# Two attention heads side by side on the column halves of the array: probabilities times v, denominators from sums, and another order in a pair

## The chip, the cores and the metric

The kernel runs on one core of a Trainium2 chip. The metric is the time on the device in microseconds (us), the median of several runs. A core has TensorE (PE, matrix products, with its weight loads as PEld), VectorE (DVE), ScalarE (ACT), GpSimd (POOL) and queues for transfers (SP is the one that loads weights). Products land in eight banks of PSUM; the other engines read them from there.

## The reference, cut to what matters

Two layers: retention and a feed-forward net, then attention and a feed-forward net, each followed by a LayerNorm with residual, for 512 tokens of 1024 channels. The change is in attention, which has 16 heads of 64 channels, and in each head three groups with dilations 1, 4 and 16:

```python
for g, (window, dil) in enumerate(DILATED_PAIRS):
    o, lse = _dilated_group(proj[0, g], proj[1, g], proj[2, g], rel_bias[...], window, dil)
    outs.append(o)
    lses.append(lse)
w = jax.nn.softmax(jnp.stack(lses, axis=0), axis=0)
o = jnp.sum(w[..., None] * jnp.stack(outs, axis=0).astype(jnp.float32), axis=0)
```

Merging the groups by their log-denominators is the same as one softmax over all keys of the three groups: sum of exp(s − m) times v, divided by the sum of exp(s − m). That is how the kernel does it.

## The kernel before, in words

**Split weights.** Every large product is done in three: a number is split into hi (a copy by ACT) and lo (the rest, by DVE), and hi·hi, hi·lo and lo·hi are added in PSUM (`mm3`). A weight arrives raw (`wraw`, SP), ACT writes `whi` (L84), DVE `wlo` (L85); this is done two tiles ahead of use, with four buffers for the halves. A tile against all tokens (`wstat`) is 8 × 3 = 24 products of 128x512 on PE.

**Attention** runs over eight pairs p of two heads, in an order that `att_schedule` writes out. The steps of a pair: *scores* of group 0, 1 and 2 (`head_mms`, the two heads on the two row halves of the array, hi and lo as above; DVE adds the position tables and keeps a running maximum `mx`); *top* for each head (PE transposes `mx`, DVE reduces it, and the maximum of each token is put on a diagonal: `diaghi` by DVE, `diaglo` by ACT, one buffer of each); *exp* for each head (two products with ones spread the maxima into a bank, DVE subtracts it from the scores in four instructions, ACT takes exps in three); *pv* (exps times v); *norm* (reciprocal of the denominator, product, split into `zhi` and `zlo`). The projections q and k of the next pair (`qk`, six weight tiles a pair) and v of the next four heads (`v`) are put between these steps, so that PE has work while DVE and ACT are at the scores. Group n = 1 and 2 of a pair need the q and k that qk 2 to 5 make, with two sets of q and k buffers that alternate (q0, k0 and q1, k1).

**pv before.** The stationary operand is 128 columns: 64 of v and 64 of ones, so that half of a bank gets the sum and the other half the denominator. A head has twelve products in float: eight over 128 columns (two groups, four residues), and four over 256, 256, 256 and 128.

**The output projection** multiplies z by two weights for each two pairs: *o*(q) fetches the weights of pairs 2q and 2q + 1, *rows*(q, b) does block b of 128 tokens (12 products of 128x512, both halves of the channels), and DVE adds the result to the residual r. The rows of pairs 0 and 1 stand in pair 4, those of pairs 2 and 3 in pair 7. The rest is done behind the loop, in `rows_product` over pairs 4 to 7, where each block's LayerNorm follows directly (`ln`: DVE statistics, POOL's power for rs at L254, ACT's scale at L281, POOL's addition at L282). The blocks are r_77 to r_80; PE transposes each (L298) for the feed-forward net, whose first products then start on halves of the tokens (128x256).

Of the kernel before, what the change touches and what calls it, by code (L numbers as in the profile page):

```python
# [7 lines left out]
F32 = mybir.dt.float32  # L8
F32R = mybir.dt.float32r
AF = mybir.ActivationFunctionType  # L10
ALU = mybir.AluOpType
# [4 lines left out]
P = 128  # L16
D = 1024
T = 512
# [6 lines left out]
HD = 64  # L25
# [7 lines left out]
RES = 4  # L33
# [1 line left out]
PH = 3 * RUN  # L35
W0, W1, W2 = (2 * RES - 1) * PH, 256, 256
WB = W0 + W1 + W2
VW = 3 * HD
S0 = 7 * P


# [56 lines left out]
def trunk(tc, a, out):  # L98
    nc = tc.nc
    plan = []  # L100

    def ret_plan(h):
        qk = [(a["w_rqk"], 4 * h + i) for i in range(4)]
        v = [(a["w_rv"], 4 * h + i) for i in range(4)]
        g = [(a["w_rg"], 4 * h + i) for i in range(4)]
        o = [(a["w_ro"], 4 * h + i) for i in range(4)]
        return qk, v, g, o

    def ffn_plan(i):
        f = 0  # L110
        for n in FC:
            plan.extend((a[f"w_up{i}"], 2 * f + j) for j in range(2 * n))
            plan.extend((a[f"w_dn{i}"], f + j) for j in range(n))
            f += n

    rp = [ret_plan(h) for h in range(RH)]
    plan += rp[0][0] + rp[0][1]
    for h in range(RH):
        plan += rp[h][2]
        if h + 1 < RH:  # L120
            plan += rp[h + 1][0] + rp[h + 1][1]
        plan += rp[h][3]
    ffn_plan(0)
    tiles = {
        "qk": lambda p, i: [(a["w_aqk"], 6 * p + i)],
        "v": lambda q, g: [(a["w_av"], 6 * q + 2 * g + i) for i in range(2 + 2 * g)],
        "o": lambda q, _: [(a["w_ao"], 2 * q + i) for i in range(2)],
    }
    first, steps = att_schedule()
    for kind, *at in first + [s for t in steps for s in t]:  # L130
        if kind in tiles:
            plan += tiles[kind](*at)
    plan += tiles["o"](2, 0) + tiles["o"](3, 0)
    ffn_plan(1)

    with tc.tile_pool(name="const", bufs=1) as cpool, tc.tile_pool(
        name="xpool", bufs=1
    ) as xpool, tc.tile_pool(name="wraw", bufs=2) as wraw, tc.tile_pool(
        name="whl", bufs=4
    ) as whl, tc.tile_pool(name="lnp", bufs=2) as lnp, tc.tile_pool(  # L140
        name="ps", bufs=8, space=PSUM
    ) as ps, tc.tile_pool(name="scratch", bufs=1, space=DRAM) as dr:
        ws = Weights(nc, plan, wraw, whl, 2, 1)
        c = Core(nc, tc, a, out, ws, cpool, xpool, lnp, ps, dr)
        c.retention()
        c.ffn(0)
        c.attention(first, steps)
        c.ffn(1)


def att_schedule():


    first = [("qk", 0, i) for i in range(4)] + [("v", 0, g) for g in range(2)]
    steps = []
    for p in range(8):
        gaps = [[("qk", p, 4), ("qk", p, 5)], [], [], [], []]
        if p < 7:
            gaps[1] += [("qk", p + 1, 0)]
            gaps[2] += [("qk", p + 1, 1)]  # L160
            gaps[3] += [("qk", p + 1, 2)]
            gaps[4] += [("qk", p + 1, 3)]
            if p % 2 and p // 2 < 3:
                for g in range(2):
                    gaps[2 + g].append(("v", p // 2 + 1, g))
        if p in (4, 7):
            q = 0 if p == 4 else 1
            gaps[1].append(("o", q, 0))
            for b, g in enumerate((1, 2, 3, 4) if p == 4 else (2, 2, 3, 4)):
                gaps[g].append(("rows", q, b))  # L170
        t = [("scores", p, 0)] + gaps[0] + [("scores", p, 1)] + gaps[1] + [("scores", p, 2)]
        t += gaps[2] + [("top", p, 0), ("top", p, 1)]
        t += gaps[3] + [("exp", p, 0)] + gaps[4]
        t += [("exp", p, 1), ("pv", p, 0), ("pv", p, 1), ("norm", p, 0)]
        steps.append(t)
    return first, steps


def residue(t, r):


    return t.rearrange("p (j r l) -> p r j l", j=NB, r=RES)[:, r]


class Core:
# [388 lines left out]
    def attention(self, first, steps):  # L574
        nc, tc = self.nc, self.tc
        with tc.tile_pool(name="at", bufs=1) as at:
            self.at = at
            self.ones = at.tile([P, P], F32R, name="ones")
            nc.vector.memset(self.ones.bitcast(F32), 1.0)
            self.vt = [at.tile([P, 12, VW], F32, name=f"v{i}") for i in range(3)]  # L580
            for v in self.vt:
                nc.gpsimd.memset(v[:, :, HD : 2 * HD], 1.0)
            self.qt, self.kt = (
                [[at.tile([P, T], F32R, name=f"{w}{i}{n}") for n in ("hi", "lo")] for i in range(2)]
                for w in "qk"
            )
            self.zs, self.wo, self.pv = {}, {}, {}
            self.tabs = {0: self.bias_tables(0)}
            n = sum(k == "qk" for k, *_ in first)
            for (_, p, i), bk in zip(first[:n], self.wstat_many(n)):  # L590
                self.att_qk(p, i, bk)
            for t in [first[n:]] + steps:
                for kind, x, y in t:
                    getattr(self, "att_" + kind)(x, y)
            tabs = [at.tile([P, 2, 4 * P], F32, name="tab", bufs=2) for _ in range(2)]
            self.ln_params(2, *[t.rearrange("p h c -> p (h c)") for t in tabs])
            self.rows_product([self.zs[p] for p in range(4, 8)], False, True)

    def bias_rows(self):

# [66 lines left out]
    def att_v(self, quad, g):  # L667


        n = 2 if g else 1  # L670
        banks = [self.bank() for _ in range(2 * n)]
        per = 4 // n
        for i in range(2 * n):
            w = self.ws.get()
            for j in range(per):
                k = per * i + j
                c = slice(j * 256 * n, (j + 1) * 256 * n)
                if g:
                    xk = [self.at.tile([P, T], F32R, name=f"xr{m}", bufs=3) for m in ("hi", "lo")]
                    for t, x in zip(xk, (self.xhi, self.xlo)):  # L680
                        self.nc.gpsimd.tensor_copy(
                            out=t.rearrange("p (r j l) -> p r j l", r=RES, j=NB),
                            in_=x[:, k, :].rearrange("p (j r l) -> p r j l", j=NB, r=RES),
# [3 lines left out]
                for b in range(NB):  # L687
                    bk = banks[b] if g else banks[b // 2]
                    o = 0 if g else b % 2 * 256
# [7 lines left out]
        for pr in range(2):  # L697
            v = self.vt[(2 * quad + pr) % 3]
            for b, bk in enumerate(banks):
                src = bk.rearrange("p (b x) -> p b x", b=2)[:, :, pr * P : (pr + 1) * P]  # L700
                dst = v[:, 4 + b : 12 : 4] if g else v[:, 2 * b : 2 * b + 2]
                for hh in range(2):
                    self.nc.scalar.activation(
                        dst[:, :, 2 * hh * HD : (2 * hh + 1) * HD],
                        src[:, :, hh * HD : (hh + 1) * HD],
                        AF.Copy,
                    )

    def head_mms(self, banks, cols, ks, qs, start, stop):

# [115 lines left out]
        tt(out=own[:, 0:3, P : 2 * P], in0=own[:, 0:3, P : 2 * P], in1=mb[:, 1:4], op=ALU.subtract)  # L826
        nc.scalar.activation(s[:, 0:S0], s[:, 0:S0], AF.Exp)

    def att_pv(self, p, h):

        bk = self.bank()
        c = slice(h * HD, h * HD + P)
        s, v = self.s[:, h], self.vt[p % 3]
        for g in (1, 2):
            for r in range(4):
                self.mm(residue(bk, r), v[:, 4 * g + r, c], residue(s[:, S0 + (g - 1) * T : S0 + g * T], r),
                        g == 1 and r == 0, False)
        for J in range(NB):
            n = 2 * P if J < 3 else P
            self.mm(bk[:, J * P : J * P + n], v[:, J, c], s[:, 2 * J * P : 2 * J * P + n], False, J == 3)  # L840
        self.pv[h] = bk

    def att_norm(self, p, _):
        nc, at = self.nc, self.at
        b0, b1 = self.pv[0], self.pv[1]
        parts = NB if p == 7 else 1
        den = at.tile([P, T], F32, name="den")
        zf = at.tile([P, T], F32, name="zf")
        hi = at.tile([P, T], F32R, name="zhi", bufs=5)
        lo = at.tile([P, T], F32R, name="zlo", bufs=5)  # L850
        nc.scalar.activation(den[0:HD], b0[HD:P], AF.Copy)
        nc.scalar.activation(den[HD:P], b1[0:HD], AF.Copy)
        for c in range(parts):
            c = slice(c * T // parts, (c + 1) * T // parts)
            nc.vector.reciprocal(out=den[:, c], in_=den[:, c])
            for bk, hs in ((b0, slice(0, HD)), (b1, slice(HD, P))):
                nc.vector.tensor_tensor(out=zf[hs, c], in0=bk[hs, c], in1=den[hs, c], op=ALU.mult)
            self.split(hi[:, c], lo[:, c], zf[:, c])
        self.zs[p] = (hi, lo)

# [120 lines left out]
```

## Time and profile before

| | us |
|---|---|
| median of 3 runs | 1708.4 (1707.71 to 1708.44) |
| profiled execution | 1707.9 |
| its span in the trace | 1705.8 |
| mean granted clock of PE | 0.997 of full |
| PE busy | 1691.8 |

The span is what the trace covers; the 2.1 us around it belong to the run's time. The clock's share is of the higher of PE's two levels, 2.4 GHz; 0.50 is 1.2 GHz.

### The profile page before, as it was taken

What the parts mean: (1) busy time and instruction counts of PE and PEld (TensorE: products, weight loads), DVE (VectorE), ACT (ScalarE), POOL (GpSimd) and SP (SyncE); (2) the same over time, 40 slices, a digit from 0 to 9 for tenths busy, and PEclk for the clock granted to TensorE, in tenths of its full rate; (3) what the DMA queues carried; (4) which work ended last, traced back from release to release, by engine and by line L of the source; (5) the groups of instructions that cost most, each with busy time, mean ns of one, the idle gap of its engine ahead of it and who ended that gap; (6) DMA issues with size and microseconds to landing.
All of it is one profiled execution on the core that took longest, in us unless ns stands there. A gap on an engine that the chain in (4) does not pass through costs nothing.

```text
span 1705.8 us, 20490 instructions
## 1 busy us (share of the span) xinstructions
PE 1691.8 (99%) x8548; PEld 1422.7 (83%) x8548; DVE 829.5 (49%) x1111; ACT 523.0 (31%) x777; POOL 188.3 (11%) x269
## 2 busy tenths in 40 slices
PE   9999999999999999999999999999999999999998
PEld 7888888888888888889888888888888888888886
DVE  6454553657433243336364564564478733233335
ACT  4322232323322122213242342432443422212221
POOL 0000000003000000017323123122100200000002
PEclk9999999999999999999999999999999999999999
DMA  7322222222223222223313223223221322223221
GB/s 275 132 74 82 73 99 76 98 74 99 99 99 99 99 99 99 98 75 115 101 58 112 75 64 110 75 87 98 76 87 62 114 90 93 99 76 122 99 99 50
DMA packets 47548, 162.52 MB, mean 95 GB/s; under 512 B 5268, under 2 KB 7316, under 8 KB 47456
## 3 DMA queue, kind: packets, MB, share of 16 engines
q1 hardware_dynamic: 42144, 155.80, 26.2%
q0 software_dynamic: 5312, 5.42, 1.8%
q8 instruction: 67, 1.10, 0.3%
q14 instruction: 25, 0.20, 0.0%
HBM read 159.02 MB, written 2.17 MB: 94 GB/s over the span
## 4 chain that ended last, share of the span: by engine, by line
PE 90%; issue 7%; DVE 2%; POOL 1%; ACT 0%; DVEq 0%; ACTq 0%; POOLq 0%
PE bank L202 89%; DVE wlo L85 1%; PE bank L298 0%; PE bank L531 0%; PE bank L784 0%; POOL r L282 0%; DVE r L284 0%; DVE r L275 0%; DVE r L317 0%; POOL rs L254 0%; DVE st L265 0%; ACT whi L84 0%; ACT r L281 0%; DVE xlo L206 0%; DVEq L974 0%
## 5 line engine op out<-in xcount | busy, mean ns | idle before, releaser
L85 DVE TENSOR_TENSOR wlo<-wraw,whi 128x1024 fp32r<-128x1024 f32 (+1 forms) x278 | 341.6, 1232 | 552.0 <-ACT whi L84 551.2
L84 ACT ACTIVATE whi<-wraw 128x1024 fp32r<-128x1024 f32 (+1 forms) x278 | 292.2, 1054 | 926.7 <-PE bank L202 602.9
L202 PE MATMUL bank<-xhi,whi 128*128 128x512 f32 (+1 forms) x1440 | 544.4, 378 | 0.0
L202 PE MATMUL bank<-xhi,wlo 128*128 128x512 f32 (+1 forms) x1440 | 540.5, 375 | 0.0
L202 PE MATMUL bank<-xlo,whi 128*128 128x512 f32 (+1 forms) x1440 | 540.0, 375 | 0.0
L202 PEld LDWEIGHTS bank<-xhi,whi 128*128 128x128 f32 x1440 | 271.4, 189 | 51.0 <-ACT xhi L205 1.5
L202 PEld LDWEIGHTS bank<-xhi,wlo 128*128 128x128 f32 x1440 | 271.0, 188 | 49.3
L202 PEld LDWEIGHTS bank<-xlo,whi 128*128 128x128 f32 x1440 | 271.2, 188 | 47.9
L202 PE MATMUL bank<-wlo,hhi 128*128 128x512 f32 x352 | 138.7, 394 | 0.0
L202 PE MATMUL bank<-whi,hhi 128*128 128x512 f32 x352 | 138.2, 393 | 0.0
L202 PE MATMUL bank<-whi,hlo 128*128 128x512 f32 x352 | 136.6, 388 | 0.0
L254 POOL TENSOR_TENSOR rs<-veps,mhalf 128x1 f32<-128x1 f32 x16 | 23.6, 1474 | 837.3 <-DVE veps L253 837.3
L564 DVE TENSOR_TENSOR ht<-ht,bank 128x512 f32<-128x512 f32 x44 | 30.3, 688 | 137.8 <-PE bank L202 137.8
L633 POOL DMA_DIRECT2D tab<-rows_dram x128 | 69.6, 551 | 218.7 <-DVE s L765 213.9
L202 PE MATMUL bank<-whi,xhi 128*128 128x512 f32 (+1 forms) x256 | 86.4, 338 | 0.0
L202 PE MATMUL bank<-wlo,xhi 128*128 128x512 f32 (+1 forms) x256 | 86.1, 336 | 0.0
L202 PE MATMUL bank<-whi,xlo 128*128 128x512 f32 (+1 forms) x256 | 86.0, 336 | 0.0
L202 PEld LDWEIGHTS bank<-whi,hhi 128*128 128x128 f32 x352 | 66.1, 188 | 15.3
L202 PEld LDWEIGHTS bank<-whi,hlo 128*128 128x128 f32 x352 | 66.1, 188 | 14.8
L202 PEld LDWEIGHTS bank<-wlo,hhi 128*128 128x128 f32 x352 | 66.2, 188 | 13.1
L317 DVE TENSOR_TENSOR r<-r,bank 128x512 f32<-128x512 f32 x56 | 37.6, 684 | 35.7 <-PE bank L202 35.7
L202 PEld LDWEIGHTS bank<-s,v 128*128 128x128 f32 x384 | 51.6, 191 | 3.2
(212 smaller groups left out, 1903.9 us busy)
## 6 DMA issues: line engine op xcount, KB each, us to landing
wraw<-in_w_up_dram SPq DMA_DIRECT2D x44, 1024.0 KB, 4.8
wraw<-in_w_dn_dram SPq DMA_DIRECT2D x22, 1024.0 KB, 4.8
wraw<-in_w_aqk_dram SPq DMA_DIRECT2D x21, 1024.0 KB, 4.8
wraw<-in_w_av_dram SPq DMA_DIRECT2D x12, 1024.0 KB, 4.8
wraw<-in_w_rv_dram SPq DMA_DIRECT2D x8, 1024.0 KB, 4.8
wraw<-in_w_rg_dram SPq DMA_DIRECT2D x8, 1024.0 KB, 5.0
wraw<-in_w_ro_dram SPq DMA_DIRECT2D x8, 1024.0 KB, 4.8
wraw<-in_w_rqk_dram SPq DMA_DIRECT2D x6, 1024.0 KB, 4.8
```

Source lines behind the costliest of these rows:

```text
L84: self.nc.scalar.activation(hi[:, c], src[:, c], AF.Copy)
L85: self.nc.vector.tensor_tensor(out=lo[:, c], in0=src[:, c], in1=hi[:, c].bitcast(F32), op=ALU.subtract)
L202: self.nc.tensor.matmul(out=out, lhsT=lhsT, rhs=rhs, start=start, stop=stop)
L254: self.nc.gpsimd.tensor_tensor(out=out, in0=veps, in1=self.mhalf, op=ALU.pow)
L317: nc.vector.tensor_tensor(out=dst, in0=dst, in1=bk, op=ALU.add)
L564: nc.vector.tensor_tensor(out=t, in0=t, in1=banks[2 * j + 1], op=ALU.mult)
L633: self.nc.gpsimd.dma_start(out=tab[r * RUN : (r + 1) * RUN, h, b * P : (b + 1) * P].rearrange("p (r l) -> p r l", r=RES), in_=src(h * WB + ...
```

## The change

Exps times v: the stationary operand is the 64 columns of a head's v, and the two heads' products alternate, head 0 into partitions 0 to 63 of a bank, head 1 into 64 to 127. The ones in v are gone. POOL adds the exps of all three groups into `esum` (three additions over both heads: 1024, 1024 and 768 columns), and one product per head with 64 columns of ones (`half`) over 512 columns puts the denominators into a second bank, on the partitions where the sums are. norm then has one reciprocal that reads PSUM and one product; ACT's two copies of the denominators are gone, as is one of two copies of each bank of v.

The order in a pair: scores 1 and 2 stand together, the first tile that was between them follows (a), the second comes ahead of the exps (b), both exps stand together, and the last two tiles of q and k of the next pair come between exp and pv (c). In pair 7 the rows of pairs 2 and 3 stand in a and b, the rows of pairs 4 and 5 (`o(2)`, `rows(2, 0..3)`) in c, and behind the loop `rows_product` covers only pairs 6 and 7.

```diff
@@ att_schedule @@
-        gaps = [[("qk", p, 4), ("qk", p, 5)], [], [], [], []]
+        a, b, c = [], [], []
         if p < 7:
-            gaps[1] += [("qk", p + 1, 0)]
-            gaps[2] += [("qk", p + 1, 1)]
-            gaps[3] += [("qk", p + 1, 2)]
-            gaps[4] += [("qk", p + 1, 3)]
+            a, b, c = [("qk", p + 1, 0)], [("qk", p + 1, 1)], [("qk", p + 1, 2), ("qk", p + 1, 3)]
...
+        if p == 4:
+            a += [("o", 0, 0)] + rows(0, 0)
+            b += rows(0, 1)
+            c += rows(0, 2, 3)
+        if p == 7:
+            a += [("o", 1, 0)] + rows(1, 0, 1)
+            b += rows(1, 2, 3)
+            c += [("o", 2, 0)] + rows(2, 0, 1, 2, 3)
+        t = [("scores", p, 0), ("qk", p, 4), ("qk", p, 5), ("scores", p, 1), ("scores", p, 2)]
+        t += a + [("top", p, 0), ("top", p, 1)] + b + [("exp", p, 0), ("exp", p, 1)]
+        steps.append(t + c + [("pv", p, 0), ("norm", p, 0)])
@@ attention @@
-            self.rows_product([self.zs[p] for p in range(4, 8)], False, True)
+            self.rows_product([self.zs[p] for p in range(6, 8)], False, True)
@@ att_pv @@
+        e = self.at.tile([P, 2, T], F32, name="esum")
+        own = self.s[:, :, 0:1024].rearrange("p h (j c) -> p h j c", c=2 * P)
+        eb = e.rearrange("p h (j c) -> p h j c", c=P)
+        tt = nc.gpsimd.tensor_tensor
+        tt(out=e, in0=self.s[:, :, S0 : S0 + T], in1=self.s[:, :, S0 + T : S0 + 2 * T], op=ALU.add)
+        tt(out=eb, in0=eb, in1=own[:, :, :, 0:P], op=ALU.add)
+        tt(out=eb[:, :, 1:4], in0=eb[:, :, 1:4], in1=own[:, :, 0:3, P : 2 * P], op=ALU.add)
+        bk, den = self.bank(), self.bank()
+        def both(out, vb, cols, start, stop):
+            for h in range(2):
+                hs = slice(h * HD, (h + 1) * HD)
+                self.mm(out(bk[hs]), v[:, vb, hs], cols(self.s[:, h]), start, stop)
...
+        for h in range(2):
+            self.mm(den[h * HD : (h + 1) * HD], self.half, e[:, h], True, True)
@@ att_norm @@
-        nc.scalar.activation(den[0:HD], b0[HD:P], AF.Copy)
-        nc.scalar.activation(den[HD:P], b1[0:HD], AF.Copy)
...
+            self.nc.vector.reciprocal(out=rec[:, c], in_=den[:, c])
+            self.nc.vector.tensor_tensor(out=zf[:, c], in0=bk[:, c], in1=rec[:, c], op=ALU.mult)
```

Three places on PE. The first is in pair 0, at the end of scores 1 (q1 and k1 are this group's operands, x and w those of a weight tile). Before:

```order
L202 MATMUL bank<-q1lo,k1hi 128x128 x2
L202 MATMUL bank<-q1hi,k1lo 128x128 x2
L202 MATMUL bank<-xhi,whi 128x512
L202 MATMUL bank<-xlo,whi 128x512
L202 MATMUL bank<-xhi,wlo 128x512
```

After:

```order
L200 MATMUL bank<-q1lo,k1hi 128x128 x2
L200 MATMUL bank<-q1hi,k1lo 128x128 x2
L200 MATMUL bank<-q0hi,k0hi 128x128 x2
L200 MATMUL bank<-q0lo,k0hi 128x128 x2
L200 MATMUL bank<-q0hi,k0lo 128x128 x2
```

The 24 products of the next pair's first tile no longer stand between scores 1 and scores 2 (q0 and k0); they follow scores 2.

The second is the exp of head 0 in pair 0 (diaghi and diaglo are the maxima on the diagonal). Before, with the second head's diaghi a whole tile of 24 products later:

```order
L202 MATMUL bank<-xhi,wlo 128x512
L202 MATMUL bank<-diaghi,ones 128x512
L202 MATMUL bank<-diaglo,ones 128x512
L202 MATMUL bank<-xhi,whi 128x512
L202 MATMUL bank<-xlo,whi 128x512
```

After:

```order
L200 MATMUL bank<-xhi,wlo 128x512
L200 MATMUL bank<-diaghi,ones 128x512
L200 MATMUL bank<-diaglo,ones 128x512
L200 MATMUL bank<-diaghi,ones 128x512
L200 MATMUL bank<-xhi,whi 128x512
L200 MATMUL bank<-xlo,whi 128x512
L200 MATMUL bank<-xhi,wlo 128x512
L200 MATMUL bank<-xhi,whi 128x512
L200 MATMUL bank<-diaglo,ones 128x512
```

The second head's diaghi now follows the first head's diaglo, and its diaglo four weight products on.

The third is the end of attention (z are the normalised heads, w the output weights, r_78 and r_79 token blocks, x the feed-forward net's input). Before, 15 products with z and 48 with x stood between these transposes of r_78 and those of r_79:

```order
L298 MATMUL bank<-ident,r_78 128x128 x8
L202 MATMUL bank<-whi,zhi 128x512
L202 MATMUL bank<-wlo,zhi 128x512
L202 MATMUL bank<-whi,zlo 128x512
L202 MATMUL bank<-whi,zhi 128x512
L202 MATMUL bank<-wlo,zhi 128x512
```

After:

```order
L296 MATMUL bank<-ident,r_78 128x128 x8
L200 MATMUL bank<-whi,zhi 128x512
L200 MATMUL bank<-wlo,zhi 128x512
L200 MATMUL bank<-whi,zlo 128x512
L200 MATMUL bank<-xhi,whi 128x256 x2
L296 MATMUL bank<-ident,r_79 128x128 x5
L200 MATMUL bank<-xlo,whi 128x256
```

Three products with z are left there instead of 15, and r_79's transposes come after two products with x.

## Rows read from the trace of the kernel before

**Rows 1.** The page, busy time and share of the span by engine.
```profile
PE 1691.8 (99%) x8548; PEld 1422.7 (83%) x8548; DVE 829.5 (49%) x1111; ACT 523.0 (31%) x777; POOL 188.3 (11%) x269
```

**Rows 2.** Windows, PE only: stretch, its length, busy (instructions), clock, DMA share, GB/s.
```profile
874.13:875.91 1.78, 1.78 (x17) 1.00 0.00 0
874.13:880.83 6.70, 6.70 (x49) 1.00 0.20 61
1272.41:1282.63 10.22, 10.22 (x46) 1.00 0.01 2
1333.73:1339.49 5.76, 5.76 (x49) 1.00 0.45 149
```

**Rows 3.** Timeline of PE, last scores of group 0: start, length, instruction, idle before.
```profile
1271.34 0.28 PE L202 MATMUL bank<-q1hi,k1lo 64*128 64x256 f32 x2
1271.46 0.23 PE L202 MATMUL bank<-q1hi,k1hi 64*128 64x128 f32 x2
...
1271.64 0.27 PE L202 MATMUL bank<-q1hi,k1lo 64*128 64x128 f32 x2
1271.84 0.50 PE L202 MATMUL bank<-xhi,whi 128*128 128x512 f32 x1
```

**Rows 4.** Timeline of PE, from weight products into scores 1 of pair 7.
```profile
1282.63 0.39 PE L202 MATMUL bank<-xhi,wlo 128*128 128x512 f32 x1
...
1282.95 0.33 PE L202 MATMUL bank<-q0hi,k0hi 64*128 64x128 f32 x2
```

**Rows 5.** Timeline of all engines, from scores 1 to scores 2 of pair 7.
```profile
1282.83 1.06 ACT L84 ACTIVATE whi<-wraw 128x1024 fp32r<-128x1024 f32 x1 [3.90 <-PE bank L202]
...
1283.92 1.23 DVE L85 TENSOR_TENSOR wlo<-wraw,whi 128x1024 fp32r<-128x1024 f32 x1 [3.58 <-ACT whi L84]
...
1284.59 0.28 PE L202 MATMUL bank<-q1lo,k1hi 64*128 64x128 f32 x2
1285.07 0.68 DVE L206 TENSOR_TENSOR k1lo<-bank,k1hi 128x512 fp32r<-128x512 f32 x1
...
1285.81 0.33 PE L202 MATMUL bank<-q1hi,k1lo 64*128 64x128 f32 x2 [0.94 <-DVE k1lo L206]
```

**Rows 6.** Windows, PE only, behind that wait; the third column from the right is the clock.
```profile
1286.00:1288.00 2.00, 2.00 (x22) 0.69 0.90 246
1288.00:1290.00 2.00, 2.00 (x6) 0.50 0.68 279
```

**Rows 7.** Timeline of all engines, exp of head 0 in pair 0.
```profile
867.73 0.39 PE L202 MATMUL bank<-diaghi,ones 128*128 128x512 f32 x1
...
868.16 0.69 DVE L801 TENSOR_TENSOR diaghi<-ident,mh 128x512 fp32r<-128x512 f32 x1 [2.23 <-PE bank L202]
...
868.72 1.26 ACT L809 ACTIVATE diaglo<-ident,m 128x128 fp32r<-128x128 f32 x4
868.77 1.28 DVE L823 TENSOR_TENSOR s<-s,bank 128x512 f32<-128x512 f32 x2
```

**Rows 8.** The page's groups: POOL's addition, count, busy us and mean ns, idle before.
```profile
L282 POOL TENSOR_TENSOR r<-r,bias 128x1024 f32<-128x1024 f32 x9 | 21.6, 2399 | 11.4 <-ACT r L281 11.4
```

**Rows 9.** Timeline of DVE, one split in the tail.
```profile
1333.16 2.58 DVE L85 TENSOR_TENSOR wlo<-wraw,whi 128x1024 fp32r<-128x1024 f32 x1 [0.43 <-ACT whi L84]
```

**Rows 10.** Timeline of all engines, the end of attention (x3 and x8 count instructions in a row).
```profile
1308.16 0.48 PE L202 MATMUL bank<-whi,zhi 128*128 128x512 f32 x1
...
1309.07 1.76 DVE L855 RECIPROCAL den<-den 128x128 f32<-128x128 f32 x2 [1.67 <-ACT den L852]
...
1318.98 1.53 POOL L254 TENSOR_TENSOR rs<-veps,mhalf 128x1 f32<-128x1 f32 x1 [115.12 <-DVE veps L253]
...
1332.26 2.40 POOL L282 TENSOR_TENSOR r<-r,tab 128x1024 f32<-128x1024 f32 x1 [1.46 <-ACT r L281]
...
1339.49 1.03 PE L298 MATMUL bank<-ident,r 128*128 128x128 f32 x8
...
1344.48 0.36 PE L202 MATMUL bank<-xhi,whi 128*128 128x256 f32 x1
```

More of the change, by code (lines that the diff above doesn't have):

```diff
@@ L37 @@
 WB = W0 + W1 + W2
-VW = 3 * HD
 S0 = 7 * P
@@ L132, in trunk @@
             plan += tiles[kind](*at)
-    plan += tiles["o"](2, 0) + tiles["o"](3, 0)
+    plan += tiles["o"](3, 0)
     ffn_plan(1)
@@ L156, in att_schedule @@
     for p in range(8):
-        gaps = [[("qk", p, 4), ("qk", p, 5)], [], [], [], []]
+        a, b, c = [], [], []
         if p < 7:
-            gaps[1] += [("qk", p + 1, 0)]
-            gaps[2] += [("qk", p + 1, 1)]
-            gaps[3] += [("qk", p + 1, 2)]
-            gaps[4] += [("qk", p + 1, 3)]
+            a, b, c = [("qk", p + 1, 0)], [("qk", p + 1, 1)], [("qk", p + 1, 2), ("qk", p + 1, 3)]
             if p % 2 and p // 2 < 3:
[L164 to L175, printed above, removed]
+                a.append(("v", p // 2 + 1, 0))
+                b.append(("v", p // 2 + 1, 1))
+        rows = lambda q, *bs: [("rows", q, i) for i in bs]
+        if p == 4:
[9 more added lines that the diff above has]
+        steps.append(t + c + [("pv", p, 0), ("norm", p, 0)])
     return first, steps
@@ L579, in attention @@
             nc.vector.memset(self.ones.bitcast(F32), 1.0)
-            self.vt = [at.tile([P, 12, VW], F32, name=f"v{i}") for i in range(3)]
-            for v in self.vt:
-                nc.gpsimd.memset(v[:, :, HD : 2 * HD], 1.0)
+            self.half = at.tile([P, HD], F32, name="half")
+            nc.vector.memset(self.half, 1.0)
+            self.vt = [at.tile([P, 12, P], F32, name=f"v{i}") for i in range(3)]
             self.qt, self.kt = (
@@ L586, in attention @@
             )
-            self.zs, self.wo, self.pv = {}, {}, {}
+            self.zs, self.wo = {}, {}
             self.tabs = {0: self.bias_tables(0)}
@@ L701, in att_v @@
                 dst = v[:, 4 + b : 12 : 4] if g else v[:, 2 * b : 2 * b + 2]
[L702 to L707, printed above, removed]
+                self.nc.scalar.activation(dst, src, AF.Copy)
     def head_mms(self, banks, cols, ks, qs, start, stop):
@@ L827, in att_exp, with att_pv @@
         nc.scalar.activation(s[:, 0:S0], s[:, 0:S0], AF.Exp)
[L829 to L833, printed above, removed]
-        for g in (1, 2):
-            for r in range(4):
-                self.mm(residue(bk, r), v[:, 4 * g + r, c], residue(s[:, S0 + (g - 1) * T : S0 + g * T], r),
-                        g == 1 and r == 0, False)
+    def att_pv(self, p, _):
+        nc = self.nc
+        e = self.at.tile([P, 2, T], F32, name="esum")
[6 more added lines that the diff above has]
+        bk, den = self.bank(), self.bank()
+        v = self.vt[p % 3]
+        def both(out, vb, cols, start, stop):
+            for h in range(2):
+                hs = slice(h * HD, (h + 1) * HD)
+                self.mm(out(bk[hs]), v[:, vb, hs], cols(self.s[:, h]), start, stop)
+        for g in (1, 2):
+            o = S0 + (g - 1) * T
+            for r in range(RES):
+                both(
+                    lambda t: residue(t, r), 4 * g + r,
+                    lambda t: residue(t[:, o : o + T], r), g == 1 and r == 0, False,
+                )
         for J in range(NB):
             n = 2 * P if J < 3 else P
-            self.mm(bk[:, J * P : J * P + n], v[:, J, c], s[:, 2 * J * P : 2 * J * P + n], False, J == 3)
-        self.pv[h] = bk
+            both(
+                lambda t: t[:, J * P : J * P + n], J,
+                lambda t: t[:, 2 * J * P : 2 * J * P + n], False, J == 3,
+            )
+        for h in range(2):
+            self.mm(den[h * HD : (h + 1) * HD], self.half, e[:, h], True, True)
+        self.pv = bk, den
     def att_norm(self, p, _):
-        nc, at = self.nc, self.at
-        b0, b1 = self.pv[0], self.pv[1]
+        at = self.at
+        bk, den = self.pv
         parts = NB if p == 7 else 1
-        den = at.tile([P, T], F32, name="den")
+        rec = at.tile([P, T], F32, name="den")
         zf = at.tile([P, T], F32, name="zf")
@@ L850, in att_norm @@
         lo = at.tile([P, T], F32R, name="zlo", bufs=5)
-        nc.scalar.activation(den[0:HD], b0[HD:P], AF.Copy)
-        nc.scalar.activation(den[HD:P], b1[0:HD], AF.Copy)
         for c in range(parts):
             c = slice(c * T // parts, (c + 1) * T // parts)
-            nc.vector.reciprocal(out=den[:, c], in_=den[:, c])
-            for bk, hs in ((b0, slice(0, HD)), (b1, slice(HD, P))):
-                nc.vector.tensor_tensor(out=zf[hs, c], in0=bk[hs, c], in1=den[hs, c], op=ALU.mult)
+            self.nc.vector.reciprocal(out=rec[:, c], in_=den[:, c])
+            self.nc.vector.tensor_tensor(out=zf[:, c], in0=bk[:, c], in1=rec[:, c], op=ALU.mult)
             self.split(hi[:, c], lo[:, c], zf[:, c])
```

## The prediction, on record before the result

> **What bounds the kernel now.** I read the page first: TensorE (PE) is busy for 1691.8 of 1705.8 us, its weight loads run beside that, and no other engine works for more than half [rows 1]. So a microsecond is gained only by taking records away from PE, and lost wherever PE must wait; what DVE, ACT and POOL do costs nothing until PE waits for it. Then I took PE's stretches one by one: first records by windows (what a product costs), then the timeline around each place where the new order puts two dependent steps closer, and last the end of attention.
>
> All times below are set against the profiled execution, 1707.9 us, 0.5 under the median of the runs (1708.4). A difference of 0.2%, 3.4 us, is about what a measurement of this kernel can tell from no change.
>
> **1. Probabilities times v.** Now a head has eight products over 128 columns and four over 256, 256, 256 and 128, and each float product is two records: 48 records a pair, 36 of 128 columns and 12 of 256. In pair 0, 16 record starts lie in 1.78 us, 0.111 each, and the pair takes 6.70, of which I count 0.09 as the switch from other products: 6.61 [rows 2]. So 12 long records take 6.61 − 36 × 0.111 = 2.61, 0.217 each, and one head alone is 3.31. In the new form a head's 24 records use one half of the array's columns and the heads alternate. No row shows column halves at work. The nearest rows are scores, where two heads lie on the two row halves: two products of 256 columns start every 0.12 us, the price of one [rows 3]: a full product of 256 columns alone costs 0.12 too, 48 starts in 5.76 [rows 2]. I take that: one head's 3.31 for both, plus one record, 0.11, by which the second head trails. The product with half-wide ones covers 512 columns, two records a head, by the lengths above an estimated 0.43 each; the first lies beside the last record of v, three follow: 3.31 + 3 × 0.43 = 4.60. Gain 2.0 a pair, **−16.1**. Bounds: 2.45 a pair if the denominators overlap as well (−19.6), and with no overlap at all 6.61 + 4 × 0.43 = 8.32 a pair, +13.7 in place of −16.1.
>
> **2. Entering and leaving halves.** From a full product to row halves takes 0.32 against 0.227 for the next full product [rows 2, 4], and the way back 0.20 against 0.12 [rows 3], 0.18 a visit. Column halves are one more visit's entry, 0.1 × 8 = **+0.8**; scores 1 and 2 side by side save a visit in seven pairs, **−1.3**. The bounds lie within 1 us.
>
> **3. Scores 2 directly behind scores 1.** The first order fence: 24 weight products (24 × 0.227 = 5.45 us) stood between them in pairs 0 to 6 and are gone. Scores 2 need k1lo, which DVE makes from the bank of qk 5. In pair 7 of before there was no such tile either, and the row shows it: ACT splits the next weight first (1.06), k1hi follows, DVE makes wlo (1.23) ahead of k1lo (0.68), and PE stands from 1284.59 to 1285.81, 1.22 where 0.12 is the pace [rows 5]. The changed order has wlo ahead of klo on DVE in every pair. So 1.1 × 7 = **+7.8**. The bound below is nothing (wlo split earlier: rival d), above it one more subtraction of DVE, 0.68, in each pair: +4.8.
>
> **4. The clock behind such a wait.** Right behind the wait in pair 7 the granted clock was 0.69 and then 0.50, the lower level of 1.2 GHz, for four microseconds: 2 × 0.31 + 2 × 0.50 = 1.6 lost, say 1.7 with the edges [rows 6]. Ahead of it PE ran 0.06 us pairs of scores and then stood for about a microsecond. I count it in four of the seven new places, **+6.8**, bounds 0 and 7 × 1.7 = 11.9.
>
> **5. The exps of both heads without a tile between.** Second order fence. There is one buffer for diaghi: the second head's can be written only when PE has read the first, 0.43 behind its start (867.73 to 868.16), and takes 0.69 [rows 7]. So the second head's first product starts at +1.18 instead of +0.46: 0.72 × 8 = 5.8. In pairs 4 and 7 an addition of a projection row stands ahead of it on DVE, about 0.7 each: **+7.2**. diaglo (1.26 on ACT from 868.72) is ready at +2.25, by when the four weight products have just run: no wait counted; if it is late by one DVE subtraction (0.64) in each pair, the bound is 12.
>
> **6. The denominators' sums on POOL.** Three additions over 1024, 1024 and 768 columns. The nearest row is POOL's addition over 1024: 2.40 [rows 8], so 2.4 + 2.4 + 1.8 = 6.6. The sums may begin when ACT has the second head's exps of groups 1 and 2: DVE's fifth and sixth subtraction at 0.64 [rows 7], plus ACT, about 6.1 after exp 0. They end at about +12.7 to 13. PE comes to the ones at 0.9 (four products of diag) + 0.7 (wait of step 5) + 48 × 0.227 + 3.4 = +15.9. Hidden, **0**, with 2.6 to spare: the cover is the two weight tiles moved to c, and PE waits once the sums need over 9.8.
>
> **7. The same sums against DVE.** In the even pairs DVE's order has the wlo of the last tile of the gap behind all eight subtractions, at about +6.2, just when POOL starts. In the tail of before such a wlo lay under a POOL addition and lasted 2.58 instead of 1.23 [rows 9]. PE would come to it at about +7.3 and wait 2.2. I cannot place the two more finely than a microsecond, so I take 1.5 of four pairs: **+3.3**, bounds 0 and 8.8.
>
> **8. The tail.** Third order fence: rows_product now has only pairs 6 and 7; 48 products of 512 columns, 48 × 0.227 = 10.9 us, went to pair 7's gap c. In that gap nothing waits for cover, so there they are +10.9. In the tail they were cover. What sets it is LayerNorm's chain: reciprocal at 1309.07, first rs at 1318.98, third POOL addition to 1334.66, 15.7 after that rs, and only then may r_79 be transposed; PE, full of products, came to it at 1339.49, and the tail from 1308.16 to the next stage is 36.3 [rows 10]. In the changed kernel the copies of the denominators are gone, so the reciprocal starts 0.25 behind the last product; DVE has three more additions in the way and four fewer products with it, +10.5 to the first rs; +15.7: r_79 at +26.4. Behind it come its transposes (0.8), 70 products of 256 columns that the list of the changed kernel shows, at 0.12 [rows 2], 8.4, and 0.8 of r_80: 36.4, with the entry 36.6. So 10.9 + 0.3 = **+11.2**, and PE's wait of some microseconds for r_79 costs one fall of the clock, **+1.7**. If the chain were as short as PE's work allows, the tail would lose its 10.9 and the clock would stay: 12.6 less.
>
> **9. What goes free.** ACT's copies of the denominators, the second copy of v, the ones in v: off PE, and hidden by its weight products. Nothing.
>
> The sum: −16.1 + 0.8 − 1.3 + 7.8 + 6.8 + 7.2 + 3.3 + 11.2 + 1.7 = **+21.4**, 1707.9 + 21.4 = 1729. Its own range: below, −3.5 (term 1), −6.8, −1.4, −3.3, −1.7, 1713; above, +5.1, +4.8, +5.5, 1745.
>
> **Rivals.** (a) *The halves run one after the other*: 8.32 against 4.60 a pair, +29.8: 1759. Against it are the scores on row halves [rows 3], for it that two heads here share the array's rows and stream through the same ones. (b) *The halves overlap, but a load of stationary values between two records doesn't hide*: 52 records a pair by half to all of 0.111, taken at half: 52 × 0.055 × 8 = +23, 1752. Full-width records of different values follow each other at 0.111 with loads between [rows 2], which speaks against it. Beside it stands the Trainium skill, page "TensorE: Matmul & The Clock Gate", section "Part 3: Packing small matmuls — row/col tiling": a load of weights overlaps running products only when the row group differs, which for column halves it does not. By that rule the time would be this rival's; the trace disagrees for full-width records on the same rows, and no row shows halves. (c) *The sums on POOL are late*, at twice the price of the row: ready at +19.3 against +15.9, 3.4 × 8 = 27, 1756. (d) *The waits are absent*, the other side: scheduling puts klo, diag and wlo early enough. Terms 3, 4, 5 and 7 fall away, −25.1: 1704. The point where it decides: all other terms sum to −3.7, so the change gains only where waits and clock cost under 0.46 us a pair. For it speaks that PE waits little anywhere now; against it [rows 5, 7], which show the two waits with their releasers.
>
> **Chances.** Forecast 0.67, (a) 0.08, (b) 0.07, (c) 0.04, (d) 0.12, others 0.02. Of (d) I count 0.08 as faster by more than 0.2% and 0.04 as the same; the forecast's lower end and the others add 0.01 and 0.02: faster 0.09, same 0.06, slower 0.85. The range 1708 to 1753 holds the forecast nearly whole, (b) and half of (d), 8 in 10.
>
> **What would show it.** Term 1: the stretch of records from s and v is 3.3 to 3.5 us and the two ones products 1.2 more. Term 3: an idle of about 1.1 before the first record with k1lo or k0lo, released by DVE. Term 4: windows at 0.50 behind it. Term 5: 0.7 before the second diaghi product. Term 6: ones products released by PE itself and not by POOL. Term 7: wlo of over 2 us in even pairs. Term 8: a wait of several microseconds ahead of r_79. Wrong it would be above all if the k and diag waits are not there, or if the halves don't run together.

## The result, and the profile after

The change makes the kernel slower: 1722.53 us (four runs, 1719.2 to 1725.95) against 1708.06 (1706.55 to 1708.44), a ratio of 1.0087 with a 95% interval of 1.0065 to 1.0108. The forecast was 1729. The profiled execution took 1723.25 with a span of 1721.4, 15.6 longer than before.

First the page of the changed kernel, busy time by engine, the line that answers to [rows 1]:

```profile
PE 1688.9 (98%) x8580; PEld 1404.8 (82%) x8580; DVE 834.2 (48%) x1109; ACT 511.0 (30%) x713; POOL 252.5 (15%) x290
```

PE is less busy than before (1688.9 against 1691.8 us) and the span is longer, so PE stands idle for 32.5 us instead of 14.0. Part of the busy time also ran at half clock: the mean granted clock is 0.989 against 0.997. The loss is waiting and low clock. The view of PE's waits in the changed kernel says what PE waited for (us in total, times, longest):

```profile
PE bank L296 <- POOL r L280: 7.0, 3, 6.1
PE bank L200 <- DVE diaghi L794: 5.2, 8, 0.9
PE bank L200 <- DVE k0lo L204: 3.7, 4, 0.9
PE bank L200 <- DVE k1lo L204: 3.7, 4, 0.9
```

Before, the same view had POOL's r once (1.5), k1lo once (0.9, the place of [rows 5]) and no diaghi. A wait in this view begins when the modelled end of the last product is reached, so it is a little shorter than what the pace loses; below I use the distances between starts.

The product with v, timeline of PE and of its weight loads (PEld) in pair 0 of the changed kernel:

```profile
879.40 0.39 PE L200 MATMUL bank<-xhi,wlo 128*128 128x512 f32 x1
879.71 3.24 PEld L200 LDWEIGHTS bank<-s,v 128*64 128x64 f32 x48 [0.35 <-issue]
879.72 3.48 PE L200 MATMUL bank<-s,v 128*64 128x128 f32 x48
883.03 1.03 PE L200 MATMUL bank<-esum,half 128*64 128x512 f32 x4
883.98 0.38 PE L200 MATMUL bank<-q1hi,k1hi 64*128 64x256 f32 x2
```

The 48 records of two heads take 3.31 us, what the prediction worked out for one head alone before, and the four with ones 0.95: 4.27 in all from the first record to the next stage, in each of the eight pairs, against 6.70 [rows 2]. Taken one by one, the records start in pairs, 7 ns apart within a pair, and each pair of 128 columns starts 0.109 after the one before. Their 48 weight loads lie in the same stretch.

The k wait, timeline of the changed kernel at scores 1 to scores 2 of pair 0, and behind it the windows of PE (the third column from the right is the clock):

```profile
848.71 1.22 DVE L84 TENSOR_TENSOR wlo<-wraw,whi 128x1024 fp32r<-128x1024 f32 x1 [3.61 <-ACT whi L83]
...
849.38 0.28 PE L200 MATMUL bank<-q0lo,k0hi 64*128 64x128 f32 x2
849.86 0.68 DVE L204 TENSOR_TENSOR k0lo<-bank,k0hi 128x512 fp32r<-128x512 f32 x1
...
850.59 0.47 PE L200 MATMUL bank<-q0hi,k0lo 64*128 64x128 f32 x2 [0.94 <-DVE k0lo L204]
```

```profile
850.60:857.40 6.80, 6.80 (x31) 0.50 0.26 82
857.40:860.00 2.60, 2.60 (x13) 0.99 0.20 29
```

It is [rows 5] again: wlo ahead of klo, PE stands 1.21 us where 0.12 is the pace. The same 1.09 is lost in all eight pairs, in pair 7 as before the change. Behind it the clock is at the lower level for 6.8 us in pairs 0 and 5 and for 3.4 in pairs 2, 3 and 7 (23.9 us in all); in pairs 1, 4 and 6 it stays up.

The exps of pair 0, timeline of the changed kernel:

```profile
866.96 0.39 PE L200 MATMUL bank<-diaghi,ones 128*128 128x512 f32 x1
...
867.18 0.40 PE L200 MATMUL bank<-diaglo,ones 128*128 128x512 f32 x1
867.38 0.69 DVE L794 TENSOR_TENSOR diaghi<-ident,mh 128x512 fp32r<-128x512 f32 x1 [2.23 <-PE bank L200]
...
868.13 0.50 PE L200 MATMUL bank<-diaghi,ones 128*128 128x512 f32 x1 [0.55 <-DVE diaghi L794]
```

Second diaghi at +1.17 (forecast +1.18); the eight places lose 0.72 to 1.09, 6.6 together. POOL's sums in pairs 0 and 2 of the changed kernel, with the wlo that starts beside the sum in pair 2:

```profile
874.14 2.45 POOL L830 TENSOR_TENSOR esum<-s 128x1024 f32<-128x1024 f32 x1 [8.57 <-ACT s L817]
876.67 3.25 POOL L831 TENSOR_TENSOR esum<-esum,s 128x1024 f32<-128x1024 f32 x1
879.99 1.83 POOL L832 TENSOR_TENSOR esum<-esum,s 128x768 f32<-128x768 f32 x1
...
999.85 3.49 POOL L830 TENSOR_TENSOR esum<-s 128x1024 f32<-128x1024 f32 x1 [5.95 <-issue]
999.86 1.22 DVE L84 TENSOR_TENSOR wlo<-wraw,whi 128x1024 fp32r<-128x1024 f32 x1
```

In pair 0 they end at 881.8 and PE comes to the ones at 883.03: hidden, by 1.2 us.

The tail of the changed kernel, PE and POOL:

```profile
1323.89 1.03 PE L200 MATMUL bank<-esum,half 128*64 128x512 f32 x4
...
1334.27 1.54 POOL L252 TENSOR_TENSOR rs<-veps,mhalf 128x1 f32<-128x1 f32 x1 [12.22 <-DVE veps L251]
...
1339.46 1.97 PE L296 MATMUL bank<-ident,r 128*128 128x128 f32 x8 [6.08 <-POOL r L280]
...
1345.67 1.09 PE L296 MATMUL bank<-ident,r 128*128 128x128 f32 x8 [0.40 <-POOL r L280]
...
1347.38 2.35 POOL L280 TENSOR_TENSOR r<-r,tab 128x1024 f32<-128x1024 f32 x1 [1.26 <-ACT r L279]
1349.79 0.77 PE L296 MATMUL bank<-ident,r 128*128 128x128 f32 x5 [0.51 <-POOL r L280]
...
1355.90 0.49 PE L296 MATMUL bank<-ident,r 128*128 128x128 f32 x3
...
1359.10 1.03 PE L296 MATMUL bank<-ident,r 128*128 128x128 f32 x8
```

The transposes are of r_77 (1339.46), r_78 (1345.67), r_79 (1349.79 and 1355.90) and r_80. From the end of the ones (1324.85) to the end of r_80's transposes (1359.89) it is 35.0 us, against 36.3 [rows 10], with 48 products fewer: PE waits for POOL's additions three times, the 6.08 us of them ahead of r_77. A window of PE shows the clock there:

```profile
1335.40:1345.50 10.10, 5.81 (x17) 0.50 0.00 0
```

**Where the time went.** Between matched starts in both traces, PE's stretches differ by: product with v and denominators −19.3 (2.43 in seven pairs, 2.26 in pair 7); scores to product with v, pairs 0 to 6, +4.99, +1.97, +3.49, +3.59, +2.14, +5.01, +1.90, together +23.1; pair 7 +12.3, of which 10.9 are the moved rows; from the last product of attention to the last product of the kernel −1.3; ahead of the first scores +0.6. That is +15.4 of the 15.6 by which the spans differ.

### The profile page after: what moved, and what is told of

It reads as the page before. It is cut to its first block, busy times and chain, and to the rows that moved or that the text cites. A ratio compares the mean times of both kernels' runs of the same rounds, so it can differ in the third digit from the quotient of the medians.

```text
span 1721.4 us, 20526 instructions
## 1 busy us (share of the span) xinstructions
PE 1688.9 (98%) x8580; PEld 1404.8 (82%) x8580; DVE 834.2 (48%) x1109; ACT 511.0 (30%) x713; POOL 252.5 (15%) x290
## 4 chain that ended last, share of the span: by engine, by line
PE 92%; issue 3%; DVE 2%; ACT 1%; POOL 1%; DVEq 0%; ACTq 0%; POOLq 0%
PE bank L200 91%; ACT whi L83 1%; DVE wlo L84 1%; POOL r L280 0%; PE bank L296 0%; PE bank L777 0%; PE bank L529 0%; DVE diaghi L794 0%; POOL rs L252 0%; ACT r L279 0%; DVE k1lo L204 0%; DVE r L282 0%; POOL esum L831 0%; DVE r L273 0%; DVE r L315 0%
## 5 line engine op out<-in xcount | busy, mean ns | idle before, releaser
L84 DVE TENSOR_TENSOR wlo<-wraw,whi 128x1024 fp32r<-128x1024 f32 (+1 forms) x278 | 347.5, 1254 | 568.1 <-ACT whi L83 567.4
L200 PEld LDWEIGHTS bank<-whi,hhi 128*128 128x128 f32 x352 | 66.1, 188 | 15.3
L315 DVE TENSOR_TENSOR r<-r,bank 128x512 f32<-128x512 f32 x64 | 42.6, 681 | 37.8 <-PE bank L200 37.8
L200 PEld LDWEIGHTS bank<-whi,xhi 128*128 128x128 f32 x256 | 48.6, 190 | 5.5 <-ACT q0hi L203 0.4
```

The costliest lines, as they stand in the source:

```text
L84: self.nc.vector.tensor_tensor(out=lo[:, c], in0=src[:, c], in1=hi[:, c].bitcast(F32), op=ALU.subtract)
L200: self.nc.tensor.matmul(out=out, lhsT=lhsT, rhs=rhs, start=start, stop=stop)
L315: nc.vector.tensor_tensor(out=dst, in0=dst, in1=bk, op=ALU.add)
```

## The experiments

**The order alone (order_only), and the halves alone (halves_only).** The order of after with the product with v of before, and the reverse:

```diff
 # order_only, against before: att_schedule and the rows behind the loop as in the change
-        t += [("exp", p, 1), ("pv", p, 0), ("pv", p, 1), ("norm", p, 0)]
+        steps.append(t + c + [("pv", p, 0), ("pv", p, 1), ("norm", p, 0)])
 # halves_only, against after: att_schedule and the rows behind the loop as before
-        steps.append(t + c + [("pv", p, 0), ("norm", p, 0)])
+        t += [("exp", p, 1), ("pv", p, 0), ("norm", p, 0)]
```

> The old product with v (48 full-width records a head pair, denominators from the ones in v), in the new order of a pair and with the new tail. Theory one (the halves earn, the order costs): the trace of the changed kernel gives 2.4 us a pair to the new product with v, 19.3 in all, so without it the order alone stands about 19 above the changed kernel: before + 34, some 1742 us, with the same eight waits of about 1.1 for k, 0.7 to 1.1 for the second diaghi, and low clock behind some of the k waits. Rival (the new sums on POOL and the halves cause the waits and the low clock): without them the waits are gone and the time is that of before plus the tail's share, about 1717.

> The new product with v and the sums on POOL, in the old order of a pair and with the old tail. If the new order were only a cost, this would be before minus 19.3: 1689 us. Theory: in the old order no tile of weights stands between the second exp and the product with v, so PE comes to the ones about 4 us after the second exp starts, while the last exps and then 8.2 us of sums (3.1 + 3.3 + 1.8 in the trace of the changed kernel) end some 12 to 14 after it: PE waits 8 to 10 us in each of eight pairs, before - 19 + 64 to 80, 1755 to 1770 us, released by POOL.

Measured: 1740.24 for the order alone (ratio 1.0207, 1.0155 to 1.0258), 1760.23 for the halves alone (1.0299, 1.0283 to 1.0314). PE's waits, of order_only and then of halves_only, and the product with v in pair 0 of halves_only:

```profile
PE bank L297 <- POOL r L281: 10.0, 3, 8.6
PE bank L201 <- DVE diaghi L800: 5.2, 8, 0.9
PE bank L201 <- DVE k1lo L205: 3.7, 4, 0.9
PE bank L201 <- DVE k0lo L205: 3.7, 4, 0.9
```

```profile
PE bank L201 <- POOL esum L833: 34.2, 8, 5.4
PE bank L201 <- ACT s L818: 10.9, 8, 2.5
PE bank L297 <- DVE r L283: 2.3, 3, 0.8
PE bank L201 <- ACT s L821: 2.1, 6, 0.4
```

```profile
874.13 0.43 PE L201 MATMUL bank<-s,v 128*64 128x128 f32 x2
875.67 2.18 PE L201 MATMUL bank<-s,v 128*64 128x128 f32 x32 [1.11 <-ACT s L818]
...
883.86 1.97 PE L201 MATMUL bank<-esum,half 128*64 128x512 f32 x4 [3.92 <-POOL esum L833]
```

The order has its waits without any sums on POOL: the rival falls, and the order, with the rows that it moves, costs about 32 us by itself (26 to 44 by the interval: the four runs lie far apart, 1736 to 1757, with mean clocks of 0.994 to 0.982, so the low clock again). With the 19.3 that the halves earn in the trace this makes +12.7, near the +14.5 of the whole change. The halves alone cost 52 us in the old order: PE comes to the ones long before the sums. A pair's product with v and ones takes 10.7 to 13.6 us there instead of 4.27, 6.4 to 9.3 more; the expectation had 8 to 10 of wait. So the tiles in c are what the halves need, and the waits between the scores and between the exps are what c was paid with. The last fence also shows whose records run together: head 1's exps come late there, and until then the two records of head 0's first product run alone, 0.16 apart; the pairs of records begin with head 1.

**Two buffers for the diagonals (diag2).**

```diff
-            d = at.tile([P, NB, P], F32R, name=f"diag{n}")
+            d = at.tile([P, NB, P], F32R, name=f"diag{n}", bufs=2)
```

> The changed kernel with two buffers for each diagonal, so that the second head's can be written before PE has read the first. Theory: the eight waits for diaghi (0.72 to 1.09 over the usual pace, 6.6 in all) go and nothing takes their place: 1722.5 - 6.6 = 1716 us, the k waits stay. Rival: DVE is late anyway (its order, not the buffer, holds diaghi back), the waits stay within 0.2 us of what they are and the time too.

Measured: 1709.05 (ten runs, 1705.98 to 1718.0; 1.0011, 0.9996 to 1.0027), 13.5 less than the changed kernel where 6.6 was expected. The wait for diaghi is gone from the view, the k waits are the same:

```profile
PE bank L296 <- POOL r L280: 7.3, 3, 6.4
PE bank L200 <- DVE k1lo L204: 3.8, 4, 0.9
PE bank L200 <- DVE k0lo L204: 3.7, 4, 0.9
```

The other 7 fit the clock: in the profiled executions, 15.1 us apart, it was low for 6.8 us in the pairs instead of 23.9, behind two of the eight k waits instead of five, and half of those 17.1 us is 8.5. Which k waits bring it down is not fixed, then, and it happened less often where the other wait of the pair was gone. The ten runs show the spread: a mean clock of 0.996 with 1705.98, 0.988 with 1718.0.

**No k wait (no_k_wait).** Scores of group 2 read the operands of group 1, so what they compute is changed; instructions and order are not.

```diff
         q, k = self.qt[n], self.kt[n]
+        if g == 2:
+            q, k = self.qt[1 - n], self.kt[1 - n]
```

> The changed kernel, but scores of group 2 read the q and k of group 1 (this changes what group 2 computes), so they don't wait for the newest k. The instructions and their order stay. Theory: the eight waits of 1.09 go, and with them the low clock that follows some of them (13.7 us at half speed over seven pairs 0 to 6 and pair 7 in the traced run, half of that lost twice over: 12 us in all): 1722.5 - 8.7 - 12 = 1702 us. Rival: the clock falls because scores 1 and 2 now follow each other without full products between them, not because of the wait: only the waits go, 1714 us, and windows at half clock stay in the pairs.

Measured: 1703.68 (nine runs, 1702.87 to 1705.24; 0.9973, 0.9963 to 0.9983). Windows of PE in the same place of pair 0, and in the tail:

```profile
849.00:857.00 8.00, 7.82 (x63) 1.00 0.21 67
1318.40:1325.10 6.70, 5.17 (x16) 0.50 0.00 0
```

In the loop of the profiled execution the clock never falls, though scores 1 and 2 still follow each other without full products between them and the diag waits (5.3) stay; all nine runs have a mean clock of 0.996 or 0.997. So the low clock in the pairs hangs on the k wait. (The 13.7 us of low clock in the expectation should read 23.9; its 12 is half of that.) Wait and clock together are worth 19 us of the changed kernel (pair 7's share of it, which the kernel before had too, included), more than the whole loss.

**The rows of pairs 4 and 5 back in the tail (tail_back).**

```diff
-            c += [("o", 2, 0)] + rows(2, 0, 1, 2, 3)
...
-            self.rows_product([self.zs[p] for p in range(6, 8)], False, True)
+            self.rows_product([self.zs[p] for p in range(4, 8)], False, True)
```

> The changed kernel with the 48 products of the rows of pairs 4 and 5 back behind the loop, so that in pair 7 nothing stands between the exps and the product with v. The prediction's step 8 (nothing in that gap waits for cover, and in the tail they are cover): 10.9 less in pair 7 and about 1.3 more in the tail, 1722.5 - 9.6 = 1713 us. Rival: in pair 7 they cover the sums on POOL, as the two tiles do in the other pairs. The sums end 14.7 after the first exp there and PE would come to the ones at about 5.6, so PE waits about 9: 1722 us, no change, with a wait released by POOL before the ones of pair 7 alone.

Measured: 1721.73 (1.0085, 1.007 to 1.01), no change. In pair 7 the stretch from the scores to the product with v is 9.9 shorter, but that product now takes 13.2 instead of 4.27, with waits that the changed kernel has not:

```profile
PE bank L199 <- POOL esum L831: 3.5, 1, 3.5
...
PE bank L199 <- ACT s L816: 1.3, 1, 1.3
```

and the low clock twice there, 6.8 us each. The moved rows are cover for the sums of pair 7, as the rival said. Pairs 0 to 6 are those of the changed kernel, yet here the clock fell in pairs 0, 1, 3, 4 and 5, for 3.4 us each, and in order_only in all eight: which pairs it falls in differs between executions.

**Three repairs together (mended)**, and then the tail as well (mended_tail). One tile goes back between scores 1 and 2, the diagonals get two buffers, and the ones and the norm of a pair come in the next one:

```diff
+        late = [("den", p - 1, 0), ("norm", p - 1, 0)] if p else []
+        t = [("scores", p, 0), ("qk", p, 4)] + late + [("qk", p, 5), ("scores", p, 1)]
+        t += a + [("scores", p, 2)] + b + [("top", p, 0), ("top", p, 1)] + c
+        t += [("exp", p, 0), ("exp", p, 1)] + d + [("pv", p, 0)]
+        steps.append(t + ([("den", p, 0), ("norm", p, 0)] if p == 7 else []))
```

> The new product with v with three repairs: one tile of weights stands between scores 1 and scores 2 again (and one at each of the next three places), the diagonals have two buffers, and the product with ones and the norm of pairs 0 to 6 come in the next pair behind its qk 4, where the sums have long ended. Theory (three causes, added): from 1722.5 the k waits 8.7, the diag waits 6.6 and the low clock in the loop 12 go, 1695 us; in the even pairs one tile of 5.4 us may not cover the last exps, up to 2 us of wait in three or four pairs, 1695 to 1703. Rival: the deferred ones hold the scores' one buffer too long, so that the next pair's scores are late by as much as is won: about 1722.

Measured: 1703.74 (ten runs, 1703.28 to 1704.77; 0.9976, 0.9966 to 0.9985). PE's waits of mended:

```profile
PE bank L300 <- POOL r L284: 7.9, 3, 6.4
PE bank L204 <- POOL xrhi L683: 1.9, 3, 0.8
PE bank L300 <- DVE r L286: 1.6, 2, 0.8
```

No wait for k, diag or the sums is left, and no low clock in the pairs. It is 9 us above the 1695 of the expectation, and about 6 of them can be placed. The ones apart from the product with v have an entry and an exit of their own (3.41 to 3.55 for the product, then about 1.1 for the ones, against 4.27 together; some 2 in all). POOL rearranges x for the tiles of v only behind the sums (1.9). The tail is 2.2 longer than that of the changed kernel, and its wait is now the largest. Of the three repairs only the two buffers were run by themselves (diag2). The second kernel, mended_tail, takes the wait in the tail away: rows of pairs 4 and 5 behind the loop, and in pair 7 alone 24 more half-wide products with ones straight from the exps, no sums.

```diff
+        if p == 7:
+            sides.append((dn, lambda vb, hs: self.half))
...
+                self.mm(out(dst[hs]), lhs(vb, hs), cols(self.s[:, h]), start, stop)
```

> The same with the rows of pairs 4 and 5 back behind the loop, and in pair 7 the denominators by half-wide ones directly from the exps (24 more products, 2.35 us more PE work) in place of the sums on POOL. Theory: 10.9 less in pair 7, 2.4 more for the ones, 1.3 more in the tail, about 2 to 3 of wait for the last exps, and the low clock in the tail gone (up to 5): 3 to 8 us below the kernel mended. Rival: the tail is bound by PE again, and the exps of pair 7 wait longer than the rows are worth: same as mended or above.

Measured: 1697.8 (four runs, 1697.54 to 1697.99; 0.9943, 0.9928 to 0.9958), 5.9 below mended and 10 below the kernel before, the fastest version here. Its waits:

```profile
PE bank L300 <- DVE r L286: 2.3, 3, 0.8
PE bank L204 <- POOL xrhi L683: 1.9, 3, 0.8
PE bank L781 <- DVE mx L774: 1.6, 1, 1.6
```

The wait for POOL in the tail is gone, and the clock is full through attention and its tail.

## Why the prediction was right, step by step

- **Terms 1 and 2, product with v: −15.3 forecast, −19.3 measured.** The halves run together, as taken from the row halves, and the denominators do too: only two of their four records count, not three. The bound of −19.6 was close. The mistake was to let the second head trail by a whole record, so that one record of ones stood alone; both heads' records start together, 7 ns apart. Rival (b), and with it the rule of the Trainium skill (page "TensorE: Matmul & The Clock Gate", section "Part 3: Packing small matmuls — row/col tiling") that loads overlap only where the row group differs, is not what the trace shows: with both heads on the same rows and other columns, and other values for each record, the 48 loads lie in the products' own stretch and the pace stays 0.109.
- **Term 3, k: +7.8 forecast, +7.6 measured** (1.09 × 7), in the place named; no_k_wait confirms that it is the wait for k. That wlo is to blame is read from the trace, and no run moves it: k0hi was ready at 849.17 and k0lo began at 849.86, behind wlo, so wlo explains 0.7 of the 1.09, and ACT's whi ahead of k0hi may be the rest. Counted in the order of the weights, that wlo is of a tile that PE reaches only at about 874.
- **Term 4, clock: +6.8 forecast, about +10 measured** in the profiled execution. It fell in four of the seven new places, as counted, but in two of them for 6.8 us instead of 3.4: 20.5 us at half speed, half of it lost. That the count was right is luck: this term differs from run to run, and in tail_back, with the same pairs, it was five of the seven.
- **Term 5, exps: +7.2 forecast, +6.6 measured**; diag2 shows the single buffer as the cause.
- **Term 6, sums hidden: right**, with less to spare. They take 7.7 to 8.8 us instead of 6.6 (3.25 for the second addition, the row used had 2.40), and the margin was 1.2 to 1.9 in seven pairs instead of 2.6.
- **Term 7, wlo against POOL: +3.3 forecast, nothing measured.** The two meet where I said, but the other way round: in pair 2 wlo and the sum started together at 999.86 and 999.85, wlo took its 1.22 and POOL's addition 3.49, against 2.45 in pair 0. Two steps failed. In the even pairs DVE was hardly the one to wait (a wlo took 1.2 to 2.2 there); and where it was, PE did not wait for it. In diag2 the wlo beside the sum took 3.41 to 3.47 in pairs 1, 2, 3 and 5, and its view of PE's waits has none for a wlo. Counted in the order of the weights, the wlo at 999.86 is not of the last tile of that gap but of a tile that PE reaches at about 1018.
- **Term 8, the tail: +12.9 forecast with its clock, +9.6 measured.** LayerNorm's chain did set it: the first rs came 9.4 behind the last product (forecast 10.5) and r_79 24.9 (forecast 26.4). But the long wait, 6.08, stood ahead of r_77 and not of r_79, where it was 0.51. The low clock (10.2 us) cost nothing that shows: some 4 us of it lay in that wait, and behind the slow products PE still waited 0.40 for r_78. One reason was wrong as well: "In that gap nothing waits for cover". tail_back shows that the sums of pair 7 do.
- The errors of terms 1, 7 and 8 (−4.0, −3.3, −3.3), 3 and 5 (−0.2, −0.6) and 4 (+3.4) leave +13.4 of the forecast's +21.4. The +15.4 between the traces is 2.0 more: 0.6 ahead of the first scores, and 1.4 about where term 2 had −1.3 for saved visits. That saving does not show: pairs 0 to 6 differ by +23.1, and k, clock and diagonals alone make 23.4. Small things such as the entry into the column halves (0.32 instead of 0.227, ahead of the product with v) may use it up. The terms for the k and diagonal waits were right by mechanism; that the whole came within 7 us is in part errors of both signs that cancel.
- **Rival (d)**, that the waits are absent, was false for the changed kernel. Its 1704 is what no_k_wait and mended show, though by other sums: in both the halves earn more than forecast, and no_k_wait keeps its diag waits. What carries over is its point: without the waits the halves earn.

What stays open is why the clock falls behind some of the k waits and not behind others of the same length, why it falls less often when the diag waits are gone, and why it does not fall behind the diag waits alone. No run here tells these apart.

## What to carry to other kernels

Two products that use half of the array's columns each cost here what one costs, so a change of that kind should be judged by what has to be ready for it: the cover that it needs was taken here from steps that needed it themselves. When PE is busy 99% of the time, list for each place where two dependent steps move together what the engine behind it does first (here a weight's split ahead of klo), and which single buffer stands between them. A consumer that waits for a slow side chain may go later in the program, as the ones did in mended; what that is worth by itself no run here shows.

## What the runs showed of the hardware

- Float products of two heads on the two column halves start in pairs 7 ns apart, every 0.109 us for 128 columns and 0.216 for 256; 48 records take 3.31 us, and going in costs 0.09 over the pace.
- One wait in which PE lost 1.1 us among short products could cost 1.7 to 3.4 us more by the granted clock (0.50 for 3.4 or 6.8 us); with the k waits taken away it stayed at 1.00 through the loop of the profiled execution.
- A POOL addition over 1024 columns took 2.40 us [rows 8] and up to 3.49 where a wlo of DVE was started with it; in pair 7 the wlo that followed lay under the addition and lasted 3.43 instead of 1.22. Either of the two can be the one that is held up: started within 0.1 us of each other, it was the addition in pairs 2, 6 and 7 of the changed kernel (3.49 against 1.22 for wlo) and wlo in pairs 1, 2, 3 and 5 of diag2 (3.4 to 3.5 against 2.40).
